# A bidirectional GLA and neighbourhood-attention layer in float32: the last two output groups as seven products of quadrant sums, and the gates' PSUM banks emptied earlier and placed elsewhere

## The chip, the cores and the metric

The kernel runs on one core of one Trainium2 chip. The metric is the device time of one execution in microseconds. The engines are named as the profile names them: PE (matmul) and PEld (its weight loads), DVE (VectorE), ACT (ScalarE), POOL (GpSimd), SP (SyncE, which issues most transfers). A number such as L480 is a line of the kernel before; the rows of the changed kernel's order carry that kernel's own line numbers.

## What is computed

One encoder layer over 1024 tokens and 16 meta tokens, width 1024, all in float32. The inner width is 2048: columns 0 to 1023 come from the gated linear attention (four heads of 256), columns 1024 to 2047 from the neighbourhood attention (sixteen heads of 64, handled as eight pairs). Cut to what matters here:

```python
u = _rmsnorm(h, norm_g)
z = u @ w_in                      # q, k, v and gates of both groups
o_gla = _rmsnorm(o_f + o_b, gla_out_norm_g) * jax.nn.silu(g_gate)
o_na  = (softmax(q k^T + bias) v) * jax.nn.silu(n_gate)
h = h + jnp.concatenate([o_gla, o_na], axis=-1) @ w_out
return h[:, N_META:]
```

Write O for `o_gla` (1024 tokens by 1024) and W for the upper 1024 rows of `w_out`. The change is in how O @ W is formed, and in the order around `g_gate` and `n_gate`.

## The kernel before, in words

Every float32 operand is split into a high part, rounded to the matmul's format, by ACT and a low part, the remainder, by DVE. `mm3` (L407) then multiplies high by high, high by low and low by high: three matmuls for each block of 128 contraction rows.

The order of the work is written out by hand. `Sched` (L65) keeps a clock of PE time as the program is written, in ns. A main generator (attention, then the four GLA heads) yields `gap` for a stretch that is to be filled, `to` for a point that the filler is to reach, `need` for something that must be done first; a filler generator (the dense projections, then `out_proj`) is stepped in between. `defer` puts a piece of work that many ns later. So the sequence on each engine is fixed when the program is built; each engine takes its instructions in that order, waiting at semaphores.

**Gates.** `dense_gate(p)` (L629) computes pair p's gate by `transposed` (L442): two halves of 512 tokens, 24 matmuls each, the second lagging the first by four blocks, each into one of the two `pd` banks of PSUM. When a half is complete, `gate_evac` (L476; its instruction is L480) empties the bank on DVE. The next user of the two `pd` banks is the following pair's projection (`pn_na`), or after the last pair the GLA queries (`pz_gz`). `k_prep(p)` (L644), part of the main generator, prepares the keys: transposes into the `pp` banks, high parts on ACT (L667), the meta keys on DVE (L670, L671), low parts on DVE (L676, four instructions), copies on POOL (L679). The queries' scores (`s`, L725 and L726) read the high and low parts. `dense_gg(h)` (L970) computes a GLA head's gate as two column halves `f`, each by `transposed`, so four banks in turn, all from `pd`. It runs as filler while `gla(h)` prepares the decays on DVE and ACT; `state` (L1148) then transposes the decayed keys (`pk`, L1152) and splits them into `kn` (L1155), which the matmuls `pu` read.

**Output.** The gated results go to a DRAM scratch `o_scr`, sixteen blocks of 128 columns. `out_proj` (L1267) runs over four groups of four blocks, in the order 2, 3 (neighbourhood attention), 0, 1 (GLA), and in each group over eight tiles of 128 tokens: SP loads 256 KB (`oin`, L1279), ACT and DVE split it (`oh`, L1298 and L1299), 2 x 12 matmuls of 512 columns multiply it by the group's weights, and DVE adds each result to `acc` (L1327), which started as the residual x. Groups 2 and 3 are the filler of the last GLA head; groups 0 and 1 run after it, and in the last one each finished half is stored.

**Weights.** `piece_split` (L247) splits one piece [128 x 512] of weights at a time, from five buffers that `piece_dma` fills, into nine pairs of buffers `wh`, `wl`. `release` lets the next piece be split when the last matmul that reads a pair is written. So in the output groups the pieces are split eight to nine ahead of their use.

Of the kernel before, what the change touches and what calls it, by code (L numbers as in the profile page):

```python
# [141 lines left out]
def kernel(  # L142
# [103 lines left out]

    def piece_split(j):  # L247
        if j < len(pieces):
            key, i, pack, a = pieces[j]
            n = a.shape[1]  # L250
            wh = wp.tile([128, 512], F32R, tag="wh", name=f"wh{j}")
            wl = wp.tile([128, 512], F32R, tag="wl", name=f"wl{j}")
            r = raw.pop(j)
            if key[0] == "o":
                act.activation(wh[:, :n], r[:, :n], AF.Copy)
                dve.tensor_tensor(wl[:, :n], r[:, :n], f32(wh[:, :n]), OP.subtract)
            for t in range(pack if key[0] != "o" else 0):
# [149 lines left out]
    def mm3(ps, ah, al, bh, bl, start, stop):  # L407
        pe.matmul(ps, ah, bh, start=start, stop=False)  # L408
        pe.matmul(ps, ah, bl, start=False, stop=False)  # L409
        pe.matmul(ps, al, bh, start=False, stop=stop)  # L410
# [232 lines left out]

    def k_prep(p):  # L644
# [16 lines left out]
        km = kmr[:, None, :].to_broadcast([128, 8, 16])
        rows = (slice(0, 64), slice(64, 128))
        for hb in range(2):
            bs = slice(4 * hb, 4 * hb + 4)
            for a in range(2):
                r = rows[a]
                act.activation(K1[a][r, bs, 0:128], srcs[hb][r], AF.Copy, scale=gk_t[r])  # L667
        for a in range(2):
            r = rows[a]
            dve.tensor_copy(K1[a][r, :, 128:BLK], km[r])  # L670
            dve.tensor_tensor(K2[a][r, :, 128:BLK], km[r], f32(K1[a][r, :, 128:BLK]), OP.subtract)  # L671
        for hb in range(2):
            bs = slice(4 * hb, 4 * hb + 4)
            for a in range(2):
                r, o = rows[a], rows[1 - a]
                dve.scalar_tensor_tensor(  # L676
                    K2[a][r, bs, 0:128], srcs[hb][r], gk_t[r], f32(K1[a][r, bs, 0:128]), OP.mult, OP.subtract
                )
# [291 lines left out]
    def dense_gg(h, between=None):  # L970
        key = ("gg", h)
        g = gpool[0].tile([128, 2, 1024], F32, tag="gt", name=f"gt{h}")
        for f in range(2):
# [290 lines left out]
        pend[1]()  # L1264


    def out_proj():  # L1267
# [14 lines left out]
        acc = {}  # L1282

        def x_in(n):
            if n < 8:
                acc[n] = zt_tile("acc0") if n == 0 else op[0].tile([128, 1024], F32, name=f"acc{n}")
                sp.dma_start(acc[n], x[n * 128 : n * 128 + 128])

        def halves(j):
            if j < len(steps):  # L1290
# [7 lines left out]
                act.activation(oh[j], t, AF.Copy)  # L1298
                dve.tensor_tensor(ol[j], t, f32(oh[j]), OP.subtract)  # L1299
# [10 lines left out]
        for j, (g, n) in enumerate(steps):  # L1310
            key = ("o", g)
            halves(j + 1)
            load(j + 3)
            x_in(j + 4)
            for f in range(2):
                ps = ps_tile("pd", f"pout{g}_{n}_{f}", 2)
                for k in range(4):
                    i = 4 * f + k
                    while (key, i) not in split:
                        pump()  # L1320
                    wh, wl, _ = split[(key, i)]
# [5 lines left out]
                dve.tensor_tensor(a, a, ps, OP.add)  # L1327
                if g == 1:
                    sp.dma_start(out[n * 128 : n * 128 + 128, f * 512 : f * 512 + 512], a)
# [145 lines left out]
```

## Time and profile before

| what | value |
|---|---|
| median of three runs | 1137.01 us (1136.85 to 1138.11) |
| profiled execution, its own time | 1136.87 us |
| its span, first to last instruction | 1134.5 us |
| mean granted clock | 0.998 |
| PE waits for DVE's `gate_evac` (weight loads) | 15.1 us, 11 times |
| bytes moved | 99.20 MB, 87 GB/s over the span |

A row of the waits reads: engine, tile and line that waited, what released it, the total in us, how often, the longest. A row of a timeline reads: start in us, length in us, engine, line, operation, output <- input, shapes; in brackets how long the engine had idled before it and what ended that. A row of a group ends with busy us, mean ns of one, and idle time before. A row of the windows gives busy us of each engine, then the granted clock, the busy share of the 16 DMA engines and GB/s. A row of the transfers gives the KB of one and the median us from issue to landing.

### The profile page before, as it was taken

The page shows a single profiled execution, that of the slowest core. Times are in us where ns is not written, and L with a number is a line of the kernel's source. Part 1 is how long each engine was busy: PE and PEld are TensorE (multiplying, and loading weights), DVE is VectorE, ACT ScalarE, POOL GpSimd, SP SyncE. Part 2 cuts the span into 40 slices and gives each one's busy share as a digit, 9 for nine tenths or more (in the row PEclk, how much of TensorE's full clock was granted, in tenths as well). Part 3 has the DMA queues.
Part 4 walks back from the last instruction along what each step waited for, and adds up shares of the span by engine and source line. Part 5 has one row for each costly group of instructions (what it writes and reads, how often), then busy time and mean ns, then how long its engine had stood idle before and what let it go on. Part 6 is the DMA issues. An engine that isn't in the chain of part 4 may idle for free.

```text
span 1134.5 us, 18937 instructions
## 1 busy us (share of the span) xinstructions
PE 1112.4 (98%) x6739; PEld 982.0 (87%) x6739; DVE 731.1 (64%) x1818; ACT 549.6 (48%) x1436; POOL 207.9 (18%) x430
## 2 busy tenths in 40 slices
PE   8999999999999999999999999999999999999998
PEld 8999898988989889898798789889879978888886
DVE  4666666676666767666664875776586577656352
ACT  6756475664656647465555542642443244313120
POOL 2633232332323223232100001001101100000000
PEclk9999999999999999999999999999999999999999
DMA  8810202112021210301124412513512364414132
GB/s 273 234 53 20 103 10 83 55 39 84 9 83 55 79 52 2 119 12 59 50 66 121 141 47 80 154 26 89 166 38 71 107 208 150 121 43 133 50 114 102
DMA packets 75621, 99.20 MB, mean 87 GB/s; under 512 B 6597, under 2 KB 46917, under 8 KB 75529
## 3 DMA queue, kind: packets, MB, share of 16 engines
q1 hardware_dynamic: 69640, 88.70, 25.1%
q0 software_dynamic: 5600, 9.18, 3.1%
q8 instruction: 53, 0.87, 0.3%
q14 instruction: 40, 0.32, 0.1%
q10 hardware_dynamic: 288, 0.14, 0.0%
HBM read 72.76 MB, written 21.04 MB: 83 GB/s over the span
## 4 chain that ended last, share of the span: by engine, by line
PE 81%; DVE 10%; ACT 4%; issue 1%; DMA 1%; POOL 1%; SPq 0%; ACTq 0%; DVEq 0%; POOLq 0%
PE pn_na L408 6%; PE pn_na L409 6%; PE pn_na L410 6%; PE pout L408 5%; PE pout L410 5%; PE pout L409 5%; PE po L797 3%; PE pp L778 3%; PE pn_gv L408 3%; PE pn_gv L409 3%; PE pn_gv L410 3%; PE pz_gz L408 3%; PE pz_gz L409 2%; PE pz_gz L410 2%; PE pz_na L410 2%; PE pz_na L409 2%
## 5 line engine op out<-in xcount | busy, mean ns | idle before, releaser
L408 PE MATMUL pn_na<-wh,uh 128*128 128x384 f32 x512 | 179.0, 350 | 9.0 <-DVE ng L480 7.1
L409 PE MATMUL pn_na<-wl,uh 128*128 128x384 f32 x512 | 173.2, 338 | 0.2 <-DVE wl L261 0.2
L410 PE MATMUL pn_na<-wh,ul 128*128 128x384 f32 x512 | 172.9, 338 | 0.0
L261 DVE SCALAR_TENSOR_TENSOR wl<-raw,gT,wh 128x256 fp32r<-128x256 f32 (+4 forms) x168 | 89.6, 571 | 38.3 <-ACT wh L260 37.3
L408 PEld LDWEIGHTS pn_na<-wh,uh 128*128 128x128 f32 x512 | 96.6, 189 | 16.6 <-DVE ng L480 9.3
L408 PE MATMUL pout<-wh,oh 128*128 128x512 f32 x256 | 103.2, 403 | 0.2 <-DVE acc L1327 0.2
L260 ACT ACTIVATE wh<-raw,gT 128x256 fp32r<-128x256 f32 (+4 forms) x168 | 87.9, 576 | 28.5 <-PE pz_gz L409 18.0
L410 PE MATMUL pout<-wh,oh 128*128 128x512 f32 x256 | 101.4, 396 | 0.0
L409 PE MATMUL pout<-wl,oh 128*128 128x512 f32 x256 | 101.3, 396 | 0.0
L409 PEld LDWEIGHTS pn_na<-wl,uh 128*128 128x128 f32 x512 | 96.9, 189 | 0.9 <-DVE wl L261 0.5
L410 PEld LDWEIGHTS pn_na<-wh,ul 128*128 128x128 f32 x512 | 96.7, 189 | 0.1
L750 ACT ACTIVATE P<-P,sm 128x384 f32<-128x384 f32 x96 | 58.5, 609 | 78.0 <-DVE sm L745 77.3
L1327 DVE TENSOR_TENSOR acc<-acc,pout 128x512 f32<-128x512 f32 x64 | 43.8, 685 | 66.7 <-PE pout L410 66.7
L213 POOL TENSOR_SCALAR post<-post 128x1 f32<-128x1 f32 x32 | 6.7, 209 | 379.4 <-ACT on L1203 379.4
L214 POOL TENSOR_TENSOR ss<-ss,epsm 128x4 f32<-128x4 f32 x64 | 74.7, 1167 | 5.3
L408 PE MATMUL pn_gv<-wh,uh 128*128 128x256 f32 (+1 forms) x256 | 75.1, 293 | 0.0
L745 DVE CUSTOM_DVE_ANT_0 P<-s,wt 128x416 f32<-128x416 f32 (+1 forms) x128 | 65.4, 547 | 12.6 <-PE s L726 11.7
L409 PE MATMUL pn_gv<-wl,uh 128*128 128x256 f32 (+1 forms) x256 | 72.7, 284 | 0.0
L410 PE MATMUL pn_gv<-wh,ul 128*128 128x256 f32 (+1 forms) x256 | 72.7, 284 | 0.0
L766 DVE TENSOR_SCALAR P<-P,sm 128x384 f32<-128x384 f32 (+1 forms) x128 | 58.3, 455 | 11.5 <-ACT P L750 0.5
L410 PEld LDWEIGHTS pout<-wh,oh 128*128 128x128 f32 x256 | 48.2, 188 | 11.7
L408 PEld LDWEIGHTS pout<-wh,oh 128*128 128x128 f32 x256 | 48.2, 188 | 11.6 <-issue 0.7
(345 smaller groups left out, 2803.8 us busy)
## 6 DMA issues: line engine op xcount, KB each, us to landing
raw<-in_w_na_dram SPq DMA_DIRECT2D x56, 256.0 KB, 3.4
v_scr<-gvst SPq DMA_DIRECT2D x64, 128.0 KB, 2.3
raw<-in_w_o_dram SPq DMA_DIRECT2D x32, 256.0 KB, 3.0
oin<-o_scr SPq DMA_DIRECT2D x32, 256.0 KB, 3.0
v<-v_scr POOLq DMA_DIRECT2D x4, 1536.0 KB, 9.4
VM<-vnat SPq DMA_DIRECT2D x8, 512.0 KB, 3.5
o_scr<-ng SPq DMA_DIRECT2D x8, 512.0 KB, 2.8
raw<-in_w_gz_dram SPq DMA_DIRECT2D x16, 256.0 KB, 2.7
```

The costliest lines, as they stand in the source:

```text
L214: pool.tensor_tensor(dst, dst, epsm[: dst.shape[0], :eng_n], OP.pow)
L260: act.activation(wh[:, ts], r[:, ts], AF.Copy, scale=g)
L261: dve.scalar_tensor_tensor(wl[:, ts], r[:, ts], g, f32(wh[:, ts]), OP.mult, OP.subtract)
L408: pe.matmul(ps, ah, bh, start=start, stop=False)
L409: pe.matmul(ps, ah, bl, start=False, stop=False)
L410: pe.matmul(ps, al, bh, start=False, stop=stop)
L745: dve.tensor_tensor_reduce(P[:, :n], ps[:, :n], wt[2 * p + a][:, off : off + n], -1.0, 3.0e38, OP.add, OP.min, mx)
L750: act.activation(loc, loc, AF.Exp, scale=-1.0, bias=mx, accum_out=sm[:, a : a + 1])
L766: dve.tensor_scalar(loc, loc, r, None, OP.mult)
L778: pe.transpose(pp[:w, c * 128 : c * 128 + 128], Ps[a][0][:, c0 : c0 + w], ident)
L797: pe.matmul(po[0][64 * a : 64 * a + 64, u4 * 128 : u4 * 128 + 128], V[:, 64 * a : 64 * a + 64], PT[a][:w, c * 128 : c * 128 + 128], start= ...
L1327: dve.tensor_tensor(a, a, ps, OP.add)
```

## The change

Four edits.

1. `k_prep` has `yield ("need", ("gate", p))` ahead of the low parts of the keys: the filler is stepped until pair p's gate is written, so its second bank's emptying stands before them on DVE. The two following gaps are shortened by the clock that this took.
2. In `dense_gg` the first column half's second bank is taken from the single `po` bank; the other three come from `pd`. `PK_NS[0]` goes from 2300 to 3500, which puts more filler ahead of the first head's first `pk`.
3. Groups 0 and 1 are no longer 2 x 8 tiles of 2 x 12 matmuls. O is cut into quadrants by token half and by group, O11 O12 / O21 O22, and W likewise by group and column half. `out_last` makes seven products of 512 x 512 x 512, each as four tiles of 12 matmuls: O11 W11; O12 W21; S1 (W11 + W12); O12' W22; S2 (T + W22); O21' (W22 + W12); -O22 (T + W21), where S1 = O21 - O22, S2 = O11 - S1, O12' = O12 - S2, O21' = O21 - O11, and T = W11 + W12 at first and T + W22 later. Partial results stay in PSUM: four banks X (`pd`, `ps`) hold the first product, which ACT also copies negated into `V`, and the second is added onto it by leaving out the clearing flag; four banks Y (`pp`, `po`, `pt`) are used in the same way for products 3 and 4, then 6 and 7.
4. The sums of weights (`T`, `U`) are made by transfers: a load of 1 MB by SP, then an accumulating transfer of 1 MB on POOL's queue (three into `T`, one into `U`). `V`, after the fifth product, goes into two quadrants of `acc` by accumulating transfers as well, eight of 256 KB, and is subtracted from a third by DVE. Sixteen loads of 256 KB fill the quadrants `r11`, `r12`, `r21`, `r22`; their memory is that of the GLA pool, which is now closed before the filler's rest is run.

```diff
-PK_NS = (2300.0, 2300.0, 2300.0, 2300.0)
+PK_NS = (3500.0, 2300.0, 2300.0, 2300.0)
...
+    for m, (g, f) in enumerate(((0, 0), (1, 0), "TT", (1, 1), "TT", "UU", "TT")):
+        add_block(("m", m), [g if g in ("T", "U") else w_o[4 * g + k, f] for k in range(4)])
...
     def dense_gate(p):
...
         silu.append((p, g))
+        S.done.add(("gate", p))
...
     def k_prep(p):
...
             dve.tensor_tensor(K2[a][r, :, 128:BLK], km[r], f32(K1[a][r, :, 128:BLK]), OP.subtract)
+        k_at[0] = S.pe
+        yield ("need", ("gate", p))
         for hb in range(2):
...
-                yield ("gap", TAIL_NS[2])
+                yield ("gap", TAIL_NS[2] - (S.pe - k_at[0] if p < NPAIR else 0.0))
...
-            yield ("gap", ATTN_NS - (TAIL_NS[2] + 1420.0 if p else 0.0))
+            yield ("gap", ATTN_NS - (TAIL_NS[2] + 1420.0 if p else S.pe - k_at[0]))
...
     def dense_gg(h, between=None):
...
-            yield from transposed(key, 128 * f, evac, pump_last=f == 1)
+            tags = (("pd", 2), ("pd", 2) if f else ("po", 1))
+            yield from transposed(key, 128 * f, evac, pump_last=f == 1, tags=tags)
...
+            if j == 9:
+                wsum["T"] = op[0].tile([128, 4, 512], F32, name="T")
+                sp.dma_start(wsum["T"], w_block(0, 0))
+            if j == 11:
+                pool.dma_start(wsum["T"], w_block(0, 1), accum_op=OP.add)
...
+    def out_last(ahead):
+        sums = {"s1": ("s1", 21, 22), "s2": ("s2", 11, "s1"), "s4": (12, 12, "s2"), "s3": (21, 21, 11)}
...
+        left = (11, 12, "s1", 12, "s2", 21, 22)
...
+        def operand(m, n):
+            t = rv(left[m], n)
+            o = op[1].tile([128, 2, 4, 128], F32R, tag="lf", name=f"lf{m}_{n}", bufs=5)
+            sign = -1.0 if m == 6 else 1.0
+            act.activation(o[:, 0], t, AF.Copy, scale=sign)
+            if m == 6:
+                dve.scalar_tensor_tensor(o[:, 1], t, -1.0, f32(o[:, 0]), OP.mult, OP.subtract)
+            else:
+                dve.tensor_tensor(o[:, 1], t, f32(o[:, 0]), OP.subtract)
+            opnd[m, n] = o
...
+        for n in range(4):
+            for q, j in ((22, (3, 3, 4, 4)), (21, (3, 3, 4, 4)), (11, (5, 5, 6, 6)), (12, (7, 7, 8, 8))):
+                todo[j[n]].append(lambda q=q, n=n: quadrant_in(q, n))
+            todo[5 + n].append(lambda n=n: add("s1", n))
+            todo[7 + n].append(lambda n=n: add("s2", n))
+            todo[9 + n].append(lambda n=n: add("s4", n))
+            todo[15 + n].append(lambda n=n: add("s3", n))
+            for m in range(2, 7):
+                todo[4 * m + n - 2].append(lambda m=m, n=n: operand(m, n))
+            todo[13 + n].append(lambda n=n: plus(11, n, X[n], store=True))
+            todo[18 + n].append(lambda n=n: [pool.dma_start(quad(q, n), V[n], accum_op=OP.add) for q in (12, 22)])
+            todo[21 + n].append(lambda n=n: plus(21, n, V[n], OP.subtract))
+            todo[21 + n].append(lambda n=n: put(12, n))
+        todo[8].append(lambda: sp.dma_start(wsum["U"], w_block(1, 1)))
+        for j, (t, g, f) in {8: ("T", 1, 1), 10: ("U", 0, 1), 16: ("T", 1, 0)}.items():
+            todo[j].insert(0, lambda t=t, g=g, f=f: pool.dma_start(wsum[t], w_block(g, f), accum_op=OP.add))
...
+        for j in range(28):
+            m, n = divmod(j, 4)
+            if j < 8:
+                ahead(16 + j)
+            for fn in todo[j]:
+                fn()
...
+            for k in range(4):
+                wh, wl = weights(("m", m), k)
+                a, b = (oh[16 + j], ol[16 + j]) if m < 2 else (opnd[m, n][:, 0], opnd[m, n][:, 1])
+                mm3(P[n], a[:, k], b[:, k], wh, wl, first and k == 0, k == 3, not first)
+                if n == 3:
+                    release(1000.0 * k)
+                yield 648
+            result(m, n)
```

DVE's order at the keys of pair 3 before; `K2` are the keys' low parts, `ng3` the pair's gate, `ng2` the gate of the pair before, which is multiplied by its attention result:

```order
L671 TENSOR_TENSOR K2_1_94<-kmr_101,K1_1_92 64x8x16
L676 SCALAR_TENSOR_TENSOR K2_0_93<-kt3_0_3194,gk_t_82,K1_0_91 64x4x128
L676 SCALAR_TENSOR_TENSOR K2_1_94<-kt3_0_3194,gk_t_82,K1_1_92 64x4x128
L676 SCALAR_TENSOR_TENSOR K2_0_93<-kt3_1_3199,gk_t_82,K1_0_91 64x4x128
L676 SCALAR_TENSOR_TENSOR K2_1_94<-kt3_1_3199,gk_t_82,K1_1_92 64x4x128
L480 TENSOR_TENSOR ng3_3103<-pz_na4_0_1_3138,rbc_87 128x4x16x8
L807 TENSOR_TENSOR ng2_2286<-po24_3055,ng2_2286 128x4x16x8
```

The same place on DVE in the changed kernel:

```order
L677 TENSOR_TENSOR K2_1_94<-kmr_101,K1_1_92 64x8x16
L483 TENSOR_TENSOR ng3_3103<-pz_na4_0_1_3138,rbc_87 128x4x16x8
L684 SCALAR_TENSOR_TENSOR K2_0_93<-kt3_0_3194,gk_t_82,K1_0_91 64x4x128
L684 SCALAR_TENSOR_TENSOR K2_1_94<-kt3_0_3194,gk_t_82,K1_1_92 64x4x128
L684 SCALAR_TENSOR_TENSOR K2_0_93<-kt3_1_3199,gk_t_82,K1_0_91 64x4x128
L684 SCALAR_TENSOR_TENSOR K2_1_94<-kt3_1_3199,gk_t_82,K1_1_92 64x4x128
L815 TENSOR_TENSOR ng2_2286<-po24_3055,ng2_2286 128x4x16x8
```

The gate's second half has moved from behind the four low parts to ahead of them; nothing else moved there, in this pair as in the seven others.

SP's queue before, some tiles into the last group; `oin` is a tile of the output's left operand:

```order
L1279 DMA oin1_3_12111<-o_scr_74 128x4x128
L1329 DMA out_0_dram<-acc0_10518 128x512 x2
L1279 DMA oin1_4_12146<-o_scr_74 128x4x128
L1329 DMA out_0_dram<-acc1_10756 128x512 x2
L1279 DMA oin1_5_12181<-o_scr_74 128x4x128
```

The same queue in the changed kernel, from the row behind the load of `oin1_2`; `r` is a quadrant's tile, `raw` a piece of weights:

```order
L1366 DMA r22_11868<-o_scr_74 128x4x128
L1366 DMA r21_11869<-o_scr_74 128x4x128
L1366 DMA r22_11868<-o_scr_74 128x4x128
L1366 DMA r21_11869<-o_scr_74 128x4x128
L246 DMA raw148_11896<-in_w_o_dram 128x512
L246 DMA raw149_11908<-in_w_o_dram 128x512
L1291 DMA oin1_3_11917<-o_scr_74 128x4x128
L1366 DMA r22_11868<-o_scr_74 128x4x128
L1366 DMA r21_11869<-o_scr_74 128x4x128
L1366 DMA r22_11868<-o_scr_74 128x4x128
L1366 DMA r21_11869<-o_scr_74 128x4x128
L1366 DMA r11_11870<-o_scr_74 128x4x128 x4
```

Where single loads and stores alternated, twelve transfers of 256 KB now come up to and with the first `r11`; behind these rows follow the four of `r12` and the 1 MB of `U`, and only then the first store.

DVE's order in the third and fourth products of the changed kernel; `rs1`, `rs2` and `r12` are the sums S1, S2 and O12', `lf2` and `lf3` the low parts of those products' operands, `wl` pieces of weights, `acc` the output:

```order
L1375 TENSOR_TENSOR rs2_11873<-r11_11870,rs1_11872 128x4x128
L1389 TENSOR_TENSOR lf2_2_12012<-rs1_11872,lf2_2_12012 128x512
L1375 TENSOR_TENSOR rs1_11872<-r21_11869,r22_11868 128x4x128
L258 TENSOR_TENSOR wl149_12026<-raw149_11908,wh149_12025 128x512
L258 TENSOR_TENSOR wl150_12036<-T_11391,wh150_12035 128x512
L1399 TENSOR_TENSOR acc4_10767<-acc4_10767,pm2_0_12018 128x512
L1375 TENSOR_TENSOR r12_11871<-r12_11871,rs2_11873 128x4x128
L1375 TENSOR_TENSOR rs2_11873<-r11_11870,rs1_11872 128x4x128
L1389 TENSOR_TENSOR lf2_3_12042<-rs1_11872,lf2_3_12042 128x512
L1399 TENSOR_TENSOR acc5_10837<-acc5_10837,pm2_1_12045 128x512
L1389 TENSOR_TENSOR lf3_0_12060<-r12_11871,lf3_0_12060 128x512
L1375 TENSOR_TENSOR r12_11871<-r12_11871,rs2_11873 128x4x128
```

Before, DVE had here per tile of 128 tokens two additions to `acc` and one low part (`oh`); now sums of quadrants, low parts of operands and of weights and additions stand in one queue. Counted to the end of an operand, the queue holds, from the first `rs2` on, 14 instructions up to `lf2_3`, 31 up to `lf3_3` and 49 up to `lf4_3`; from the first low part that reads `U` to `lf4_3` it holds 22.

More of the change, by code (lines that the diff above doesn't have):

```diff
@@ L233 @@
         add_block(("gg", h), [w_gg[h, k] for k in range(4)], 2)
-    for g in (2, 3, 0, 1):
+    for g in (2, 3):
         add_block(("o", g), [w_o[4 * g + k, f] for f in range(2) for k in range(4)])
-    raw = {}
+    for m, (g, f) in enumerate(((0, 0), (1, 0), "TT", (1, 1), "TT", "UU", "TT")):
+        add_block(("m", m), [g if g in ("T", "U") else w_o[4 * g + k, f] for k in range(4)])
+    raw, wsum = {}, {}
     split = {}
@@ L240, in piece_dma @@
     def piece_dma(j):
-        if j < len(pieces):
+        if j < len(pieces) and not isinstance(pieces[j][3], str):
             a = pieces[j][3]
@@ L249, in piece_split @@
             key, i, pack, a = pieces[j]
-            n = a.shape[1]
+            n = 512 if isinstance(a, str) else a.shape[1]
             wh = wp.tile([128, 512], F32R, tag="wh", name=f"wh{j}")
             wl = wp.tile([128, 512], F32R, tag="wl", name=f"wl{j}")
-            r = raw.pop(j)
-            if key[0] == "o":
+            r = wsum[a][:, i] if isinstance(a, str) else raw.pop(j)
+            if key[0] in "om":
                 act.activation(wh[:, :n], r[:, :n], AF.Copy)
                 dve.tensor_tensor(wl[:, :n], r[:, :n], f32(wh[:, :n]), OP.subtract)
-            for t in range(pack if key[0] != "o" else 0):
+            for t in range(pack if key[0] not in "om" else 0):
                 ts = slice(t * (n // pack), (t + 1) * (n // pack))
@@ L404, in u_meta, with mm3 @@
             S.defer(ns, fn)
[L407 to L410, printed above, removed]
+    def mm3(ps, ah, al, bh, bl, start, stop, more=False):
+        pe.matmul(ps, ah, bh, start=start, stop=False, skip_group_check=more)
+        pe.matmul(ps, ah, bl, start=False, stop=False, skip_group_check=more)
+        pe.matmul(ps, al, bh, start=False, stop=stop, skip_group_check=more)
     def first_pair(key, c1, hook):
@@ L448, in transposed @@
             if k == 0:
-                ps[half] = ps_tile("pd", f"pz_{key[0]}{key[1]}_{c0}_{half}", 2)
+                ps[half] = ps_tile(tags[half][0], f"pz_{key[0]}{key[1]}_{c0}_{half}", tags[half][1])
             while (key, k) not in split:
@@ L1264, in gla @@
         pend[1]()
+    acc, oh, ol, op = {}, {}, {}, []
+    steps = [(g, n) for g in (2, 3) for n in range(8)] + [(g, n) for g in (0, 1) for n in range(4)]
+    R = {}
     def out_proj():
-        steps = [(g, n) for g in (2, 3, 0, 1) for n in range(8)]
-        ld, oh, ol = {}, {}, {}
-        op = []
+        ld = {}
         def load(j):
@@ L1299, in halves, with ahead @@
                 dve.tensor_tensor(ol[j], t, f32(oh[j]), OP.subtract)
+        def ahead(j):
+            halves(j + 1)
+            load(j + 3)
         for j in range(2):
@@ L1309, in out_proj @@
             x_in(j)
[L1310 to L1313, printed above, removed]
+        for j, (g, n) in enumerate(steps[:16]):
+            ahead(j)
             x_in(j + 4)
+            if j == 9:
[3 more added lines that the diff above has]
+                pool.dma_start(wsum["T"], w_block(0, 1), accum_op=OP.add)
             for f in range(2):
@@ L1317, in out_proj @@
                 for k in range(4):
[L1318 to L1321, printed above, removed]
+                    wh, wl = weights(("o", g), 4 * f + k)
                     mm3(ps, oh[j][:, k], ol[j][:, k], wh, wl, k == 0, k == 3)
@@ L1327, in out_proj, with weights, w_block, out_tiles @@
                 dve.tensor_tensor(a, a, ps, OP.add)
-                if g == 1:
-                    sp.dma_start(out[n * 128 : n * 128 + 128, f * 512 : f * 512 + 512], a)
+        yield from out_last(ahead)
+    def weights(key, i):
+        while (key, i) not in split:
+            pump()
+        return split[(key, i)][:2]
+    def w_block(g, f):
+        return w_o[4 * g : 4 * g + 4, f].rearrange("k p c -> p k c")
+    def out_tiles(tp):
+        for q in (22, 21, 11, 12, "s1", "s2"):
+            R[q] = tp.tile([128, 4, 512], F32, name=f"r{q}")
+        wsum["U"] = tp.tile([128, 4, 512], F32, name="U")
+        op.append(tp)
@@ new lines, in rv, with quadrant_in, add, quad @@
+    def rv(q, n):
+        return R[q][:, :, 128 * n : 128 * n + 128]
+    def quadrant_in(q, n):
+        h, g = q // 10 - 1, q % 10 - 1
+        ts = slice(512 * h + 128 * n, 512 * h + 128 * n + 128)
+        sp.dma_start(rv(q, n), o_scr[4 * g : 4 * g + 4, :, ts].rearrange("f p t -> p f t"))
+    def out_last(ahead):
+        sums = {"s1": ("s1", 21, 22), "s2": ("s2", 11, "s1"), "s4": (12, 12, "s2"), "s3": (21, 21, 11)}
+        def add(s, n):
+            d, a, b = (rv(q, n) for q in sums[s])
+            dve.tensor_tensor(d, a, b, OP.subtract)
+        left = (11, 12, "s1", 12, "s2", 21, 22)
+        opnd = {}
+        def operand(m, n):
[8 more added lines that the diff above has]
+            opnd[m, n] = o
+        V = [op[0].tile([128, 512], F32, name=f"V{n}") for n in range(4)]
+        def quad(q, n):
+            return acc[n + 4 * (q // 10 - 1)][:, 512 * (q % 10 - 1) : 512 * (q % 10)]
+        def plus(q, n, src, sign=OP.add, store=False):
+            a = quad(q, n)
+            dve.tensor_tensor(a, a, src, sign)
+            if store:
+                put(q, n)
+        def put(q, n):
+            b = n + 4 * (q // 10 - 1)
+            sp.dma_start(out[b * 128 : b * 128 + 128, 512 * (q % 10 - 1) : 512 * (q % 10)], quad(q, n))
+        X, Y = {}, {}
+        tags = ((("pd", 2), ("pd", 2), ("ps", 2), ("ps", 2)), (("pp", 2), ("pp", 2), ("po", 1), ("pt", 1)))
+        todo = {j: [] for j in range(28)}
+        for n in range(4):
[14 more added lines that the diff above has]
+            todo[j].insert(0, lambda t=t, g=g, f=f: pool.dma_start(wsum[t], w_block(g, f), accum_op=OP.add))
+        def result(m, n):
+            if m == 0:
+                act.activation(V[n], X[n], AF.Copy, scale=-1.0)
+            elif m == 2:
+                plus(22, n, Y[n])
+            elif m == 3:
+                plus(12, n, Y[n])
+            elif m == 4:
+                dve.tensor_tensor(V[n], V[n], X[n], OP.add)
+            elif m == 5:
+                plus(22, n, Y[n], store=True)
+            elif m == 6:
+                plus(21, n, Y[n], OP.subtract, True)
+        for j in range(28):
[4 more added lines that the diff above has]
+                fn()
+            P = X if m in (0, 1, 4) else Y
+            if m in (0, 2, 4, 5):
+                tag, bufs = tags[P is Y][n]
+                P[n] = ps_tile(tag, f"pm{m}_{n}", bufs)
+            first = m in (0, 2, 4, 5)
+            for k in range(4):
[6 more added lines that the diff above has]
+            result(m, n)
@@ L1363 @@
     S.flush()
+    gstack.close()
+    out_tiles(ostack.enter_context(tc.tile_pool(name="tp", bufs=1)))
     while S.step_filler():
@@ L1366 @@
     S.flush()
-    gstack.close()
     ostack.close()
```

4 lines of the change are left out of this document (2 added, 2 removed).

## The prediction

> **What bounds the kernel now.** I read the page's busy table first, then the waits, then timelines of three places, then the tail.
>
> ```profile
> span 1134.5 us, 18937 instructions
> PE 1112.4 (98%) x6739; PEld 982.0 (87%) x6739; DVE 731.1 (64%) x1818; ACT 549.6 (48%) x1436; POOL 207.9 (18%) x430
> PEclk9999999999999999999999999999999999999999
> core 0: us, PE busy (x) PEld busy (x) DVE busy (x) ACT busy (x) POOL busy (x), PEclk, DMA share, GB/s
> 990.00:1130.00 140.00, 140.00 (x624) 113.20 (x623) 66.44 (x119) 24.91 (x50) 4.73 (x10) 1.00 0.29 89
> ```
>
> PE is busy for 1112.4 of 1134.5 us at a full clock, and in the last 140 us without a gap. So only two things shorten the span: fewer PE instructions, or fewer of the 22 us in which PE waits. The second comes from the waits of PE's weight loads, which show a stall from its start (the matmul before still drains in PE's own row):
>
> ```profile
> PEld po L797 <- issue: 12.0, 56, 0.4
> PEld pn_na L408 <- DVE ng L480: 9.3, 7, 1.6
> PEld pz_gg L408 <- DVE gt L480: 3.7, 3, 1.9
> PEld pz_gz L408 <- DVE ng L480: 2.1, 1, 2.1
> ```
>
> The last three rows all wait for `gate_evac` (L480), 15.1 us together: a `pd` bank is wanted while DVE has not emptied it.
>
> **Part 1: gates ahead of the keys' low parts.** One of the eight places, DVE and then the weight loads:
>
> ```profile
> 268.08 3.04 DVE L676 SCALAR_TENSOR_TENSOR K<-kt,gk_t,K 64x512 fp32r<-64x512 f32 x4
> 271.15 0.69 DVE L480 TENSOR_TENSOR ng<-pz_na,rbc 128x512 f32<-128x512 f32 x1
> 271.76 0.68 DVE L807 TENSOR_TENSOR ng<-po,ng 128x512 f32<-128x512 f32 x1
> 274.02 0.44 DVE L745 CUSTOM_DVE_ANT_0 P<-s,wt 128x272 f32<-128x272 f32 x1 [1.25 <-PE s L726]
> 270.26 0.19 PEld L409 LDWEIGHTS pn_na<-wl,uh 128*128 128x128 f32 x1
> 270.43 0.19 PEld L410 LDWEIGHTS pn_na<-wh,ul 128*128 128x128 f32 x1
> 271.90 0.19 PEld L408 LDWEIGHTS pn_na<-wh,uh 128*128 128x128 f32 x1 [1.28 <-DVE ng L480]
> 272.01 0.19 PEld L409 LDWEIGHTS pn_na<-wl,uh 128*128 128x128 f32 x1
> 273.40 0.19 PEld L725 LDWEIGHTS s<-K,Q 128*128 128x128 f32 x1
> ```
>
> The four low parts (3.04 us) stand in front of the emptying of the gate's second bank. Loads come every 0.17 us, so the one at 272.01 would have come at 270.77: 1.24 us lost, 0.04 less than the wait's 1.28. After the change the gate is emptied from 268.08 to 268.77, 1.8 us before PE wants the bank, so this wait goes whole. PE's own order does not change in these eight places. Removed: 9.3 + 2.1 = 11.4 us, less 8 x 0.05 = 11.0.
>
> What is late next: the four low parts end 0.69 us later, at 271.85, and the first scores read them. Their load came at 273.40 and will be wanted at 273.40 - 1.24 = 272.16. That leaves 0.3 us. In the first pair, where the wait was 1.6, PE comes earlier still; I take 0.2 us off for it. Behind the low parts stands L807, which moves 0.1 us, and DVE then idles 1.25 us before the scores' row (274.02), so the delay dies there. **10.8 us gained**; bounds 11.0 and 5.5 (8 x 0.69 given back).
>
> **Part 2: a second gate bank elsewhere.** In `dense_gg` the first half's second bank moves from `pd` to `po`, so the second half no longer waits for it: 3.7 us in three waits. But DVE's own chain is close behind. The place in head 2, where 1.54 us was waited:
>
> ```profile
> 823.58 0.19 PEld L408 LDWEIGHTS pz_gg<-uh,wh 128*128 128x128 f32 x1 [1.54 <-DVE gt L480]
> 827.10 1.22 DVE L1098 SCALAR_TENSOR_TENSOR ga<-ga,gk 128x1024 f32<-128x1024 f32 x1
> 830.76 0.28 DVE L1155 TENSOR_TENSOR kn<-pk,kn 128x128 fp32r<-128x128 f32 x1
> 829.29 0.27 PE L1152 MATMUL pk<-ident,ga 128*128 128x128 f32 x1
> 831.84 0.28 PE L410 MATMUL pu<-v,kn 128*128 128x256 f32 x1
> ```
>
> PE will reach the transpose `pk` at 829.29 - 1.5 = 827.8, but DVE finishes its input at 828.32: 0.6 us is waited there instead, and 0.2 more for `kn` (ready at 831.04, wanted by the third `pu` at 831.84 - 0.9). So 0.7 of 1.5 us stays. `PK_NS[0]`, raised by 1200, puts two more filler units ahead of head 0's `pk`, so PE has work there, but also a weight split ahead of `kn`. I take the same share of 3.7: **1.5 us gained**, bounds 0 and 3.6.
>
> **Part 3: seven products.** The last two groups before, one tile of 12 matmuls after another:
>
> ```profile
> 1091.45 0.69 DVE L1327 TENSOR_TENSOR acc<-acc,pout 128x512 f32<-128x512 f32 x1 [2.13 <-PE pout L410]
> 1097.07 0.69 DVE L1327 TENSOR_TENSOR acc<-acc,pout 128x512 f32<-128x512 f32 x1 [2.12 <-PE pout L410]
> 1130.80 0.69 DVE L1327 TENSOR_TENSOR acc<-acc,pout 128x512 f32<-128x512 f32 x1 [2.12 <-PE pout L410]
> 1131.52 0.33 SPq L1329 DMA_DIRECT2D out_dram<-acc  x1
> L256 DVE TENSOR_TENSOR wl<-raw,wh 128x512 fp32r<-128x512 f32 x15 | 10.3, 690 | 0.4 <-ACT wh L255 0.2
> L1299 DVE TENSOR_TENSOR oh<-oin,oh 128x512 fp32r<-128x512 f32 x20 | 13.7, 685 | 0.7 <-ACT oh L1298 0.7
> L1298 ACT ACTIVATE oh<-oin 128x512 fp32r<-128x512 f32 x20 | 12.3, 629 | 55.6 <-PE pout L410 51.0 <-DMA oin<-o_scr 4.7
> ```
>
> Two tiles take 1097.07 - 1091.45 = 5.62 us, a tile 2.81. There are 32 tiles (2 groups x 8 x 2); seven products make 28. Four tiles fewer: **11.2 us**, and the phase lasts 28 x 2.81 = 78.7 us if PE never waits. The tail (an add of 0.69 us and a store of 256 KB) stays as it is.
>
> The cover is DVE and the DMA. From the first `s2` sum (`rs2` in the order) to the low part of the fifth product's last operand (`lf4_3`) DVE has 49 instructions of 0.69 us, 33.8 us. That operand is wanted 19 tiles and two matmuls in, at 53.9 us, so `s2` must start by 20.1 us after the phase's start or PE waits for the difference. ACT has fewer instructions at 0.63 and is not the limit. `s2` needs the first `r11` quadrant. What came before on SP:
>
> ```profile
> oin<-o_scr SPq DMA_DIRECT2D x32, 256.0 KB, 3.0
> v<-v_scr POOLq DMA_DIRECT2D x4, 1536.0 KB, 9.4
> vx<-v_scr POOLq DMA_DIRECT2D x4, 512.0 KB, 9.9
> 907.55 0.89 POOL L1031 DMA_DIRECT2D v<-v_scr  x1 [0.27 <-DMA oin<-o_scr]
> K<-in_c_mask_dram POOLq DMA_DIRECT2D x2, 256.0 KB, 6.9
> 908.00:918.00 10.00, 10.00 (x46) 8.09 (x45) 5.10 (x8) 4.75 (x10) 1.15 (x2) 1.00 1.04 318
> ```
>
> The core's DMA engines are full at 318 GB/s (share 1.04), so 256 KB take 0.8 us, and landing takes 2.2 more. SP passes the wait of the `oin1_2` load about 8 us into the phase; then 12 transfers of 256 KB (3.15 MB) up to the first `r11`: 9.9 us, landed at 20.1. Exactly in time, if nothing else moves. But the second accumulate into `T` may start on POOL's queue as soon as the old `T` is read, about step 5 (14 to 15 us). By 15 us 2.2 MB have gone; the other 0.92 MB at half the rate take 5.8: landed at 23.0, 2.9 us late.
>
> No trace here shows an accumulating transfer. The nearest row is `v`, on the same queue: 1536 KB in 9.4 us. The slow end is the mask's 256 KB in 6.9. With bytes counted once, U's sum is complete at 38.9 us (7.1 MB at 318 from 8 us on, 2.2 to land, then 0.9 to issue as with `v`, 3.3 to move, 2.2 to land), and DVE's 22 instructions from U's first split to `lf4_3` end at 54.1: no further stall. I take **3 us** for the stall; bounds 0 and some 11. The gain of the products is then 8.2.
>
> Sum: 10.8 + 1.5 + 8.2 = 20.5 us. The profiled execution took 1136.87 us, 2.4 around its span, and 0.14 under the median of the runs: 1116.4, rounded to **1116.5**.
>
> **The rivals.**
> (a) No stall (0.25): the two queues' transfers fit side by side, SP gets ahead. 11.2 + 10.8 + 1.5: 1113.4. For it: DMA at 0.29 in the last 140 us before. Against: 19 loads of 256 KB and 1 MB of `U` are put close together.
> (b) An accumulate reads its target too (0.2), so its bytes count twice. 8.1 MB are moved before `U` lands at 35.8, its accumulate ends at 45.5, and 22 DVE instructions (15.2) later it is 60.7 instead of 53.9: a stall of 7, 1120.4.
> The Trainium skill, Collectives: The Full Stack, section "The bandwidth ceiling: the fold count and why AG ≠ RS ≠ AR", says that an add in the DMA path needs two source reads and ran at about half the rate of a copy; by that rule this case would be the one, and no run here shows it yet.
> (c) The gates' gain halves (0.06): the low parts of the keys, 0.69 us later, are waited for in every pair, since only 0.3 us is spare: 1136.9 - 5.5 - 1.5 - 8.2 = 1121.7.
> (d) Slower (0.07): accumulates are slow. POOL's queue carries T, U, T and eight `V` transfers, 5.24 MB, between 14 us and the last tile. Below 62 GB/s (84.7 us) the queue alone takes the phase to 14 + 84.7 + 3.5 = 102 us, and the whole 23.5 us are gone. At 49 GB/s, a quarter of what `v` and `vx` reach together (2.1 MB in 0.89 + 9.9 us), the phase takes 124.5: 1159. For it stands only the mask's row (38 GB/s, in the crowded start), against it `v`'s.
>
> My forecast has 0.42, between 1114 and 1120.
>
> **The numbers.** 0.2% of 1137 us is 2.3 us, about what a measurement of this kernel tells from no change. All cases but (d) are far below that: faster 0.92, same 0.01, slower 0.07. The range runs from 1112 (no stall, and 3 us in part 2) to 1127 (accumulates at some 80 GB/s); beyond it lie (d) and little else.
>
> **What would show it.** In the new profile: no wait of `pn_na` or `pz_gz` for `ng`; three waits of `pz_gg` gone and new ones of `pk` or `pu` for DVE under 2.5 us; 48 matmuls fewer; in the last 82 us a few waits of PE for `lf`, the largest around the third and fourth products, and DVE idle for an `r11` load just before. The forecast is wrong if PE waits in the last phase for over 6 us, or if the scores wait for `K`.

## The result and the profile after

The changed kernel takes 1119.66 us (median of four executions, 1118.37 to 1120.16), the kernel before 1136.93: the ratio is 0.9842, 95% interval 0.9827 to 0.9857, or 18.0 us (16.3 to 19.7); the two medians lie 17.3 apart. The forecast was 1116.5 within 1112 to 1127. The profiled execution is the fastest of the four, 1118.37 us, 18.5 under the profiled one of before, where the sum said 20.5.

The first two lines of the page of the changed kernel, which answer to those of before (1112.4 us of PE, 6739 matmuls):

```profile
span 1116.6 us, 18945 instructions
PE 1099.4 (98%) x6691; PEld 970.7 (87%) x6691; DVE 750.4 (67%) x1854; ACT 564.5 (51%) x1464; POOL 220.7 (20%) x442
```

48 matmuls fewer, and still 98% busy. In its waits the three rows for `gate_evac` (`ng`, `gt`) are gone. New or larger rows at the places that were changed are these (engine, tile, line, releaser, total us, times, longest); what else grew lies in the first 50 us:

```profile
PEld pm L413 <- DVE lf L1389: 5.9, 4, 2.2
PEld po L411 <- DVE ah L1247: 2.8, 3, 1.4
PEld pu L413 <- DVE kn L1164: 1.5, 3, 0.6
PEld pm L411 <- ACT lf L1385: 0.6, 1, 0.6
```

To see where the time came from, take rows that stand at the same place of the program in both kernels: the first transpose of the meta keys (`kmt`), the last scores (`s`), the first and the last work of the GLA state (`pk`, `pu`). Each row gives durations, then the start of the first and of the last matmul of its kind. Before:

```profile
L649 PE MATMUL kmt<-ident,kvm x8: 230/230/231, 55.3 to 536.0; 16*128 16x16 f32 x8
L726 PE MATMUL s<-K,Q x128: 285/351/355, 67.8 to 594.8; 128*128 128x416 f32 x96, 128*128 128x272 f32 x32
L1152 PE MATMUL pk<-ident,ga x56: 270/271/276, 637.2 to 1014.4; 128*128 128x128 f32 x56
L410 PE MATMUL pu<-v,kn x44: 276/282/387, 639.8 to 1025.4; 128*128 128x256 f32 x44
```

After:

```profile
L655 PE MATMUL kmt<-ident,kvm x8: 230/230/231, 55.7 to 527.3; 16*128 16x16 f32 x8
L734 PE MATMUL s<-K,Q x128: 285/351/355, 66.6 to 584.2; 128*128 128x416 f32 x96, 128*128 128x272 f32 x32
L1161 PE MATMUL pk<-ident,ga x56: 270/271/276, 626.3 to 1002.4; 128*128 128x128 f32 x56
L413 PE MATMUL pu<-v,kn x44: 276/281/388, 629.3 to 1013.4; 128*128 128x256 f32 x44
```

| stretch | before, us | after, us | change | forecast |
|---|---|---|---|---|
| start to first `kmt` | 55.3 | 55.7 | +0.4 | 0 |
| first `kmt` to last `s` | 539.5 | 528.5 | -11.0 | -10.8 (part 1) |
| last `s` to last `pu` | 430.6 | 429.2 | -1.4 | -1.5 (part 2) |
| last `pu` to the end | 109.1 | 103.2 | -5.9 | -8.2 (part 3) |

They add up to the 17.9 us between the spans (1134.5 - 1116.6). Two parts came as forecast. The third is 2.3 us short, so the phase of the products is the place to look.

Its first and last matmul, from PE's timeline:

```profile
1028.24 0.40 PE L411 MATMUL pm<-wh,oh 128*128 128x512 f32 x1
1112.39 0.39 PE L413 MATMUL pm<-wh,lf 128*128 128x512 f32 x1
```

84.15 us from start to start, where 28 tiles of 2.81 less one matmul of 0.23 make 78.4: 5.7 us lost. In between, on DVE, POOL and the weight loads (in brackets the idle time before and what ended it):

```profile
1055.02 0.69 DVE L1375 TENSOR_TENSOR rs<-r,rs 128x512 f32<-128x512 f32 x1 [6.40 <-DMA r<-o_scr]
1074.19 0.69 DVE L258 TENSOR_TENSOR wl<-U,wh 128x512 fp32r<-128x512 f32 x1 [2.84 <-ACT wh L257]
1075.99 0.69 DVE L1389 TENSOR_TENSOR lf<-r,lf 128x512 fp32r<-128x512 f32 x1
...
1043.04 1.33 POOL L1426 DMA_DIRECT2D T<-in_w_o_dram  x1 [13.53 <-DVE wl L258]
1063.68 1.28 POOL L1426 DMA_DIRECT2D U<-in_w_o_dram  x1 [19.31 <-DMA U<-in_w_o_dram]
...
1056.37 0.19 PEld L413 LDWEIGHTS pm<-wh,lf 128*128 128x128 f32 x1 [2.21 <-DVE lf L1389]
1063.59 0.19 PEld L413 LDWEIGHTS pm<-wh,lf 128*128 128x128 f32 x1 [1.58 <-DVE lf L1389]
1076.73 0.19 PEld L413 LDWEIGHTS pm<-wh,lf 128*128 128x128 f32 x1 [1.70 <-DVE lf L1389]
```

DVE idles twice: 6.40 us for the first `r11`, and at 1074.19 for ACT, which had waited for `U`'s sum. PE's waits lie right behind: at 1056 to 1064, for the last three operands of the third product, and at 1074 to 1077, for the last one of the fourth. With two shorter ones (0.38 at 1059.38, 0.58 at 1074.73) they make 6.5 us. The second group was not in the forecast's likeliest case. What the transfers did, from the windows (the last three columns are the granted clock, the busy share of the DMA engines and GB/s) and the groups of transfers (KB each, median us to landing):

```profile
1058.00:1062.00 4.00, 4.00 (x18) 3.00 (x17) 4.00 (x8) 1.26 (x3) 0.00 (x0) 1.00 1.06 357
1066.00:1070.00 4.00, 4.00 (x19) 3.19 (x18) 4.00 (x7) 2.28 (x5) 0.00 (x0) 1.00 1.03 164
...
T<-in_w_o_dram POOLq DMA_DIRECT2D x3, 1024.0 KB, 9.1
U<-in_w_o_dram SPq DMA_DIRECT2D x1, 1024.0 KB, 6.2
U<-in_w_o_dram POOLq DMA_DIRECT2D x1, 1024.0 KB, 9.8
```

From 1058 to 1062 plain loads fill the engines and move 357 GB/s. From 1066 to 1070 `U`'s accumulate is alone; the engines are just as full (1.03) and move 164, 0.46 of that (the profile counts an accumulate's bytes once: three of 1 MB show as 3.14 MB on their queue). This is the price of rival (b). The Trainium skill, Collectives: The Full Stack, section "The bandwidth ceiling: the fold count and why AG ≠ RS ≠ AR", puts an add (there in the reduce step of a collective) at two source reads and about half a copy's rate; the rate in this trace agrees, with 164 against 357 GB/s, while the reads themselves it does not show.

My account after this reading, theory A: the three parts add up; in the last phase `r11` costs some 4 us and `U` some 2.3, both late because accumulates use the transfer engines for twice the time. Rivals: the gates gave less and the products more; so many loads in so short a time would be late without any accumulate; DVE has too much to do there.

### The profile page after: what moved, and what is told of

It reads as the page before. It is cut to its first block, busy times and chain, and to the rows that moved or that the text cites. A ratio compares the mean times of both kernels' runs of the same rounds, so it can differ in the third digit from the quotient of the medians.

```text
span 1116.6 us, 18945 instructions
## 1 busy us (share of the span) xinstructions
PE 1099.4 (98%) x6691; PEld 970.7 (87%) x6691; DVE 750.4 (67%) x1854; ACT 564.5 (51%) x1464; POOL 220.7 (20%) x442
## 4 chain that ended last, share of the span: by engine, by line
PE 83%; DVE 6%; ACT 3%; DMA 3%; SPq 2%; issue 1%; POOL 1%; DVEq 0%; POOLq 0%; ACTq 0%
PE pn_na L411 7%; PE pn_na L413 6%; PE pn_na L412 6%; PE po L805 4%; PE pp L786 3%; PE pn_gv L411 3%; PE pn_gv L413 3%; PE pn_gv L412 3%; PE pz_gz L411 3%; PE pz_na L413 3%; PE pz_na L412 3%; PE pz_na L411 3%; PE pz_gg L411 3%; PE pz_gz L412 3%; PE pz_gz L413 3%; PE pz_gg L412 3%
## 5 line engine op out<-in xcount | busy, mean ns | idle before, releaser
L1212 ACT ACTIVATE on<-po 128x256 f32<-128x256 f32 x32 | 12.3, 383 | 89.6 <-PE po L413 89.4
L772 DVE RECIPROCAL sm<-sm 128x1 f32<-128x1 f32 x128 | 20.8, 162 | 53.3 <-POOL sm L760 49.0
L411 PE MATMUL pz_na<-uh,wh 128*128 128x512 f32 x128 | 53.2, 416 | 0.0
L411 PE MATMUL pout<-wh,oh 128*128 128x512 f32 x128 | 52.3, 409 | 0.2 <-DVE acc L1341 0.2
L411 PE MATMUL pz_gz<-uh,wh 128*128 128x512 f32 x128 | 52.5, 410 | 0.0
L786 PE MATMUL pp<-ident,P 128*128 128x128 f32 (+1 forms) x384 | 52.5, 272 | 0.0
```

The costliest lines, as they stand in the source:

```text
L411: pe.matmul(ps, ah, bh, start=start, stop=False, skip_group_check=more)
L772: dve.reciprocal(r, s)
L786: pe.transpose(pp[:w, c * 128 : c * 128 + 128], Ps[a][0][:, c0 : c0 + w], ident)
```

## The experiments

### The parts one by one

**Gates alone** is the kernel before with these lines and the two gaps shortened as in the changed kernel:

```diff
+        S.done.add(("gate", p))
...
+        k_at[0] = S.pe
+        yield ("need", ("gate", p))
         for hb in range(2):
```

> The kernel before with edit 1 alone (the pair's gate ahead of the keys' low parts). Theory A (the parts add, and the gates are worth what their waits were): no weight load of pn_na or pz_gz waits for ng, 10.8 to 11.0 us gained, 1126.0 us. Rival B (the gates give only half, and the rest of what the whole change gained, 17.3 us, comes from the products without a stall): 5.5 us gained, 1131.4.

Measured: 1125.85 us, ratio 0.9902 (0.9888 to 0.9915), 11.1 us gained (9.7 to 12.7). Its rows for the same two places, and what is left of the waits for `gate_evac`:

```profile
L652 PE MATMUL kmt<-ident,kvm x8: 230/230/232, 56.3 to 527.9; 16*128 16x16 f32 x8
L731 PE MATMUL s<-K,Q x128: 285/351/355, 67.3 to 584.9; 128*128 128x416 f32 x96, 128*128 128x272 f32 x32
...
PEld pz_gg L408 <- DVE gt L480: 3.7, 3, 1.9
```

From the first `kmt` to the last `s` it takes 528.6 us, as in the changed kernel (528.5). Rival B is out.

**Bank alone, with and without the longer `PK_NS[0]`:**

```diff
-PK_NS = (2300.0, 2300.0, 2300.0, 2300.0)
+PK_NS = (3500.0, 2300.0, 2300.0, 2300.0)
...
+            tags = (("pd", 2), ("pd", 2) if f else ("po", 1))
+            yield from transposed(key, 128 * f, evac, pump_last=f == 1, tags=tags)
```

> The kernel before with edit 2 alone (po as the second bank of a GLA gate's first half, and the longer time ahead of the first pk). Theory A: the 3.7 us of pz_gg go, some 2.2 to 2.5 of them come back as waits of pk and pu for DVE or as other waits of that stage: 1.2 to 1.5 us gained, 1135.4 to 1135.7. Rival B: all of it is gained, 1133.2. Rival C: nothing, since DVE's chain is the limit there, 1136.9.

> The kernel before with the bank of edit 2 but without the longer time ahead of head 0's first pk. Theory A: in head 0 PE meets DVE's chain up to 1.2 us earlier, and waits 0.5 to 1 us there: 1136.0 to 1136.5. Rival: the time ahead of pk is worth nothing by itself, the same as with both, 1135.5.

Measured: with both 1135.24 us, ratio 0.9984 (0.9975 to 0.9992), 1.8 us gained (0.9 to 2.8); without the longer time 1135.02, ratio 0.9983 (0.9975 to 0.9992), the same. The waits that came in place of the 3.7 us, first with it, then without:

```profile
PEld po L408 <- DVE ah L1239: 2.9, 3, 1.4
PEld pu L410 <- DVE kn L1156: 1.5, 3, 0.6
```

```profile
PEld pk L1153 <- issue: 1.3, 1, 1.3
PEld po L408 <- DVE ah L1239: 1.0, 2, 0.6
```

Before, `po` waited 1.2 us, `pu` 1.0 and `pk` 0.2. So with the longer time some 2.2 us come back on `po` and `pu`, and without it 1.1 on `pk` (where the profile names nothing that it waited for). The first shows what becomes of a freed wait; the number in `PK_NS` only chooses where the rest is waited, and theory A's half a microsecond for it is not there.

**Products alone** is the changed kernel without those two edits, the two gaps as they were.

```diff
-        k_at[0] = S.pe
-        yield ("need", ("gate", p))
...
-PK_NS = (3500.0, 2300.0, 2300.0, 2300.0)
+PK_NS = (2300.0, 2300.0, 2300.0, 2300.0)
...
-            tags = (("pd", 2), ("pd", 2) if f else ("po", 1))
+            tags = (("pd", 2), ("pd", 2))
```

> The kernel before with edits 3 and 4 alone (seven products, gates and banks as before). Theory A: four tiles of 2.81 us go and PE waits some 6.5 us for operands of the third to fifth products, as in the changed kernel: 4.7 to 5.9 us gained, 1131 to 1132.2. Rival B (the stall belongs to the whole change, since earlier gates leave DVE or the transfers behind): 11.2 us gained, 1125.7.

Measured: 1131.52 us, ratio 0.9947 (0.9932 to 0.9962), 6.0 us gained (4.3 to 7.7). That is close to theory A's 4.7 to 5.9: the stall belongs to the products. 11.1 + 1.8 + 6.0 = 18.9, against 18.0 (16.3 to 19.7) for all three: they add, as far as this can tell.

### What the stall is made of

**Accumulates as plain transfers.** This kernel leaves out three of the four sums of weights (the expectation says two): `T` after the third product and after the fifth, and `U`, are overwritten.

```diff
-            todo[j].insert(0, lambda t=t, g=g, f=f: pool.dma_start(wsum[t], w_block(g, f), accum_op=OP.add))
+            todo[j].insert(0, lambda t=t, g=g, f=f: pool.dma_start(wsum[t], w_block(g, f)))
```

> The changed kernel, but the three transfers into T and U in the last phase (T, U, T) overwrite instead of adding: same bytes, same queue, same order, so two of the four sums of weights are left out. Theory A (an accumulating transfer takes its bytes twice from the transfer engines, and this is what makes r11 and U late): each of the first two takes some 3.3 us less of them, r11 comes 3 us and U's block 6 us earlier, the stall of 6.5 us falls to 1 to 3, 1114 to 1116. Rival B (bytes count once, the stall comes from so many loads in so short a time): no change, 1119 to 1120. Rival C (DVE has too much to do there): no change either.

Measured: 1113.62 us, ratio 0.9796 (0.9783 to 0.9809), clear of the changed kernel's interval: 5.2 us from ratio to ratio, 4.3 in the phase of the profiled executions (79.86 for 84.15). One wait for an `lf` is left; the engines, as full as before, move more; and the same megabyte lands sooner:

```profile
1062.64 0.19 PEld L413 LDWEIGHTS pm<-wh,lf 128*128 128x128 f32 x1 [1.32 <-DVE lf L1389]
...
1050.00:1054.00 4.00, 4.00 (x19) 3.23 (x18) 0.23 (x1) 1.83 (x3) 0.00 (x0) 1.00 1.10 362
...
U<-in_w_o_dram POOLq DMA_DIRECT2D x1, 1024.0 KB, 5.6
```

In the changed kernel the window from 1050 to 1054, with the loads and `T`'s accumulate, had 247 GB/s at a share of 1.11. It is the adding in the transfers that costs, not the number of loads, and not DVE, whose work is the same. A second read as its reason fits the rate, but no run separates it from anything else that an add may need.

**The quadrants sooner, `U` early, and both.** In the first, six quadrants go ahead of the `oin` load on whose buffer SP waits, `r11` beside the others, and `r12` and `U`'s load two steps earlier:

```diff
-            for q, j in ((22, (3, 3, 4, 4)), (21, (3, 3, 4, 4)), (11, (5, 5, 6, 6)), (12, (7, 7, 8, 8))):
+            for q, j in ((22, (3, 3, 4, 4)), (21, (3, 3, 4, 4)), (11, (3, 3, 4, 4)), (12, (5, 5, 5, 5))):
...
-        todo[8].append(lambda: sp.dma_start(wsum["U"], w_block(1, 1)))
+        todo[6].append(lambda: sp.dma_start(wsum["U"], w_block(1, 1)))
...
+            if j == 3:
+                for fn in todo[j]:
+                    fn()
             if j < 8:
                 ahead(16 + j)
-            for fn in todo[j]:
+            for fn in todo[j] if j != 3 else []:
```

> The changed kernel with the quadrants' loads in another order: six of them ahead of the third oin load of the second product, on whose buffer SP waits; r11 next to r22 and r21 and not behind them; then r12 and U two steps earlier. Theory A (r11 and U late on the queue): r11 lands by some 1046 instead of 1054.5, U's accumulate starts 3 to 7 us earlier, the stall falls by 4 to 6, 1114 to 1116. Rival B (the transfer engines are full from 1038 to 1062 whatever the order): what r11 gains r22 and r21 lose, 1 us at most gained, 1118.5 to 1120. Rival C (DVE): no change.

In the second, `U` is loaded and summed during the last GLA head, where `T`'s first sum is made (its load and accumulate in the last phase are gone):

```diff
                 sp.dma_start(wsum["T"], w_block(0, 0))
+                wsum["U"] = op[0].tile([128, 4, 512], F32, name="U")
+                sp.dma_start(wsum["U"], w_block(1, 1))
             if j == 11:
                 pool.dma_start(wsum["T"], w_block(0, 1), accum_op=OP.add)
+                pool.dma_start(wsum["U"], w_block(0, 1), accum_op=OP.add)
```

> The changed kernel with U loaded and summed where T's first sum is made, during the last GLA head. Theory A (two separate lateness terms, r11 some 4 us and U some 2.3): only the second goes, 1.7 to 2.8 us gained, 1117 to 1118. Rival B (the wait for U is the only one that costs, the earlier ones are made up for later): 5 us or more, 1114. Rival C (DVE's queue, still behind after r11, would be late with U in place too): under 0.5 gained, 1119.5.

The third has both edits.

> The changed kernel with both: the quadrants' loads sooner, and U summed during the last GLA head. Theory A: nearly the whole stall of 6.5 us goes, 1113 to 1114.5. Rival B (the transfer engines): some 3 us, 1116.5. Rival C (DVE's 64 us of work in the phase is the limit): a wait of 2 us or more for lf stays with DVE never idle before it, 1115.5 or more.

Measured, with the phase from its first to its last matmul's start in the profiled execution (one each; each ratio is to executions of the kernel before that were taken beside that kernel's):

| kernel | median, us | ratio to before (95%) | phase, us |
|---|---|---|---|
| changed | 1119.66 | 0.9842 (0.9827 to 0.9857) | 84.15 |
| quadrants sooner | 1119.33 | 0.9848 (0.9835 to 0.9862) | 83.17 |
| `U` early | 1115.80 | 0.9815 (0.9801 to 0.9828) | 82.04 |
| both | 1114.65 | 0.9799 (0.9785 to 0.9812) | 79.07 |
| accumulates plain | 1113.62 | 0.9796 (0.9783 to 0.9809) | 79.86 |

Sooner quadrants alone gain nothing by the ratios and 1.0 us in the phase, against theory A's 4 to 6 and within the 1 us of rival B. The waits of that kernel, DVE and then the weight loads:

```profile
1057.31 0.69 DVE L1375 TENSOR_TENSOR rs<-r,r 128x512 f32<-128x512 f32 x1 [2.54 <-DMA r<-o_scr]
1074.15 0.69 DVE L258 TENSOR_TENSOR wl<-U,wh 128x512 fp32r<-128x512 f32 x1 [4.73 <-ACT wh L257]
...
1061.66 0.19 PEld L413 LDWEIGHTS pm<-wh,lf 128*128 128x128 f32 x1 [0.90 <-DVE lf L1389]
1074.69 0.19 PEld L411 LDWEIGHTS pm<-wh,lf 128*128 128x128 f32 x1 [2.48 <-ACT lf L1385]
1076.69 0.19 PEld L413 LDWEIGHTS pm<-wh,lf 128*128 128x128 f32 x1 [1.71 <-DVE lf L1389]
```

The wait for `r11` (`rs<-r,rs`) is gone, one of 2.54 us for a quadrant of S1 (`rs<-r,r`) is there in its place, and PE's at 1056 is gone. But DVE splits `U` 45.0 us after the phase's start, where it was 46.0: SP issued its load at 28.1 instead of 28.4, since all sixteen quadrants still stand ahead of it and the transfer engines were full (shares of 1.05 and 1.13 from 1040 to 1060). So DVE waits 4.73 us for `U` instead of 2.84, and PE 2.48 instead of 0.58. What PE no longer loses at the first wait it loses at the second: from `U`'s split to the phase's last matmul it is 38.2 us in both kernels. With `U` early the first group stays, and with both nearly nothing:

```profile
PEld pm L413 <- DVE lf L1391: 4.1, 3, 2.1
```

```profile
PEld pm L413 <- DVE lf L1391: 0.8, 1, 0.8
...
1062.00:1066.00 4.00, 3.66 (x17) 2.93 (x16) 4.00 (x8) 1.45 (x3) 0.00 (x0) 1.00 0.03 6
1066.00:1070.00 4.00, 4.00 (x19) 3.26 (x18) 4.00 (x7) 2.25 (x5) 0.00 (x0) 1.00 0.00 0
```

The first fence is of the kernel with `U` early, the second of the one with both. There the transfer engines stand idle from 1062 to 1070 and DVE is busy throughout; the wait of 0.76 us that is left, at 1062.40, is DVE's, well under rival C's 2. `U` early gained 2.1 us in the phase and 3.1 by the ratios, where theory A had 1.7 to 2.8. By the phases, `r11` alone costs 82.04 - 79.07 = 3.0 us, `U` alone 83.17 - 79.07 = 4.1, and both together 84.15 - 79.07 = 5.1, not their sum of 7.1. "Both" is faster than the changed kernel: the intervals of the ratios do not overlap, while those of `U` early and the changed kernel just touch. Against "`U` early" its gain is 3.0 us in the profiled phases, while the ratios' intervals overlap.

## Why the prediction was right, and where it was not

**Part 1** held in size and mechanism: 11.0 us in its stretch and 11.1 (9.7 to 12.7) alone, for 10.8. The place shown in the prediction looks like this now:

```profile
264.39 0.69 DVE L483 TENSOR_TENSOR ng<-pz_na,rbc 128x512 f32<-128x512 f32 x1
265.00 3.07 DVE L684 SCALAR_TENSOR_TENSOR K<-kt,gk_t,K 64x512 fp32r<-64x512 f32 x4
...
268.46 0.19 PEld L733 LDWEIGHTS s<-K,Q 128*128 128x128 f32 x1
```

The low parts end at 268.07, and the first scores' load comes 0.39 us later without a wait; the working gave that margin 0.3. It was enough, and no row of the waits has the scores waiting for `K`, so rival (c) fell. (The gate's row starts 0.61 us ahead of the low parts, as at 271.15 and 271.76 in the prediction. The working took the row's length of 0.69 for that distance; the difference is what the margin gained.)

**Part 2** held: 1.4 us in its stretch and 1.8 (0.9 to 2.8) alone, for 1.5. That part of the wait returns on DVE's chain is shown, 2.1 us of it in the changed kernel (1.6 more at `po`, 0.5 more at `pu`), within the 2.5 that the prediction allowed. But it named `pk` and `pu`, and most of it lies at `po`, which waits for `ah`; the wait of `pk` appears only without the longer `PK_NS[0]`.

**Part 3** had the four tiles right and the stall too small: 5.1 us for 3 (84.15 less the 79.07 of "both"; 5.7 above 28 tiles without a wait). The step that failed is "With bytes counted once, U's sum is complete at 38.9 us". ACT's first split of `U` started at 1073.5, 45.3 us after the phase's start; rival (b), with the accumulates' bytes counted twice, said 45.5. `U`'s accumulate alone took 9.8 us from issue to landing, where the forecast had 6.4 and rival (b) 9.7. The plain transfers, with `U`'s first split 4.9 us sooner in the phase, show that the adding is the cause. So the mechanism was that of (b), held at 0.2, and of its stall of 7 us 5.1 came: its time of 1120.4 is nearer to the median of 1119.66 than the forecast's 1116.5, which the range made good. The prediction also called itself wrong if PE waited over 6 us in the last phase: by the rows of the weight loads it waited 6.5, by the phase's length 5.7.

The steps before it held: SP issued the first quadrant 8.8 us after the start (8 forecast), and `T`'s accumulate followed at 14.8 (14 to 15). `r11` was later than worked out (the sum that needs it started at 26.8, landing was put at 23.0); the working counted the accumulate's bytes once there too, and with plain transfers that sum started at 24.3. That its stall alone, 3.0 us with `U` early, is still the one forecast is luck. DVE's rows of 0.69 us start 0.60 apart (three in a row at 1061.05, 1061.65 and 1062.25), so the 49 instructions to `lf4_3` take 29.5 us and not 33.8, and `s2` could start by 24.4 instead of 20.1: the later landing and the faster queue nearly cancel. (Rival (b)'s 7, with its 22 rows counted in the same way, would be 4.9.) And PE did not wait for `lf4_3` at all, but for the third product's operands, the first of them directly behind that sum in DVE's queue.

The same slip lay in the working on `U`: I asked only when the fifth product's last operand is ready. The low part that PE waited for (at 1076.73) is of the fourth product, and stands three DVE instructions behind the first split of `U` in the same queue. In a queue in order, each operand behind a late instruction has to be set against the time at which it is wanted, the nearest ones first.

The sign was never near: rival (d) needed accumulates below 62 GB/s, and `U`'s alone ran at 164. Rival (a), no stall, gave 1113.4; with the two late transfers out of the way the kernel takes 1114.65, and with plain transfers 1113.62.

## What to carry to other kernels

A sum made by a transfer is not free of the transfer engines: here an accumulating transfer's bytes had to be counted twice, so do that sum with them doubled, and make it where the engines have room, as `U`'s sum was here during the last GLA head. Two late inputs on one in-order engine do not add: removing the first alone may give next to nothing, so look in the new profile at which wait has grown, and try both together. When a wait on PE is taken away by moving work on another engine, work out the margin of what is pushed back (0.3 us here, and 0.39 measured): that tells a full gain from half of one.

## What the runs showed of the hardware

Issuing an accumulate of 1 MB took POOL 1.28 to 1.33 us, the plain transfer of the same shape 0.75 to 0.83. That is some 0.5 us apiece; of the 4.2 us by which `U`'s accumulate landed later than the plain transfer (9.8 for 5.6) the other 3.7 are not POOL's.

A short pause of PE may cost its clock as well. In the profiled execution of "products alone", PE waited 2.06 us; then came matmuls of 0.63 us at a distance of 0.43 for some 3 us, where 0.39 and 0.23 are usual, and the granted clock of the window is 0.86:

```profile
1068.94 0.50 PE L413 MATMUL pm<-wh,lf 128*128 128x512 f32 x1 [2.06 <-DVE lf L1387]
1070.42 0.63 PE L411 MATMUL pm<-wh,lf 128*128 128x512 f32 x1
...
1070.00:1080.00 10.00, 10.00 (x39) 7.89 (x38) 10.00 (x18) 4.13 (x8) 1.28 (x1) 0.86 0.57 177
1090.00:1100.00 10.00, 10.00 (x38) 8.00 (x37) 10.00 (x18) 4.72 (x8) 0.52 (x1) 0.83 0.57 158
```

A second such stretch, the last row, follows a wait of 1.27 us that ends at 1089.62. The changed kernel, where PE's own rows show waits of 1.77 and 1.28 us at the same two places, kept a clock of 1.00:

```profile
1056.37 0.50 PE L413 MATMUL pm<-wh,lf 128*128 128x512 f32 x1 [1.77 <-DVE lf L1389]
1076.73 0.50 PE L413 MATMUL pm<-wh,lf 128*128 128x512 f32 x1 [1.28 <-DVE lf L1389]
```

The Trainium skill, TensorE: Matmul & The Clock Gate, section "Why this matters for your kernels", names idle gaps of over some 3 us as what puts the clock back; here gaps of 2.06 and 1.27 us were followed by a lower clock in one execution, and one of 1.28 in another was not. Whether the gaps are the cause, and why the two differ, no run here shows.
